# Moving the last mLSTM head ahead of the gate pairs, and keeping one output unit's partial result in SBUF, in a decoder layer's kernel

## The chip, the cores and the metric

The kernel runs on one core of a Trainium2 chip. The metric is the device time of one execution in microseconds (us). Engines are named as the profile names them: PE (TensorE, matmuls), PEld (its weight loads), DVE (VectorE), ACT (ScalarE), POOL (GpSimd), SP (SyncE, which only issues DMAs here).

## The reference, cut to what matters

One layer over 1024 positions of width 2048, all in float32: a combined projection, a sparse attention over a latent (group A), an mLSTM of four heads (group B), the output projection, and a norm.

```python
p = x @ W_in                        # 7512 columns: q, k, v, gates, indexer, ...
# group A: indexer picks the top 256 causal keys of each query,
#   h_A = softmax(q_lat . c_sel + bias) . c_sel      8 heads,  y_A = h_A * silu(z_A)
# group B, 4 heads, chunk by chunk (state C):
#   q, k = silu(conv(.)); S = (q k^T) * D
#   num = S v + inter * (q C);  C = f C + (k w)^T v
#   y_B = norm(num / den) * sigmoid(o) * silu(z)
y = concat(y_A, y_B) @ W_out        # 2048 x 2048
out = LayerNorm(alpha * x + y)
```

## The kernel before, in words

**Matmuls.** Each float32 operand is split into a high and a low part, rounded for the engine (`split`: a cast on ACT writes `..h`, a subtraction on DVE writes `..l`), and a product is three matmuls (high.high, high.low, low.high). The big projections are done as products of 2 x 2 blocks with sums of blocks, seven products for eight: `a11, a12, a22, s1..s4` are blocks and sums of the moving operand, `b11, b21, t1, t2, b22, t3, t4` those of the weights.

**Input projection.** 19 *units* (`Unit`) of two column groups each ("a pair") go through two passes over the inner dimension. A unit of either pass is 84 matmuls of 512 columns on PE. The first pass stores its part of the result in DRAM (`part_d`). The second pass loads that part into a tile `res` (L622), adds its seven products there (`add`, L676), and hands `res` on. `res` is an x_tile: one of a ring of 16 buffers (tag `xs`) that also holds the split blocks of x. A buffer is taken again when what used it last is done.

**Order of the second pass.** `sequence` lists the units head by head. For each of the four mLSTM heads there is a unit with its q and k, two *gate pairs* (output gate and SiLU gate, 256 columns) and some *other pairs*, which belong to the attention: `G_QA` pairs (queries, scaled on ACT at L893 and stored to `qa_d`) and `G_ZA` pairs (SiLU on ACT at L237, stored to `gate_a`). `shares` deals the seven other pairs out: 2, 2, 1, 2. The function `mlstm` runs the q/k unit and the convolutions, then units from its `queue` until two are left (*front* units, in which `mlstm_half` makes transposes, scores and their splits), then the two halves of the chunk recursion, each with one unit beside it. The small matmuls of a chunk (`num`, `up`) are put between the unit's 84 by `after(m)`, which holds an instruction back until the m-th of the unit's marks (a mark stands behind every sixth matmul, 14 to a unit). With heads 0 to 2 the two last units are the gate pairs, with head 3 they are two other pairs. After head 3 come `latent` (loads and splits the latent, `ch`, `cl`), `keys(0)` (`kps`: keys of attention head 0), `queries(0)` and `stores(3)` (transposes `ht` of the last head's result and its store), and then the attention, with nothing of the projection left beside them.

**Output projection.** `Product(p, c)` is one half of the inner dimension (p) for one half of the output columns (c), again seven products of 48 matmuls. There are four quarters: `unit_0` = (0,0), `unit_1` = (0,1), `unit_2` = (1,0), and a tail for the last, tile by tile of 128 rows, done in the plain way. The quarters with p = 0 store their result to DRAM (`z_d`). Those with p = 1 load x into `z` (L1375, L1490), scale it by alpha on ACT (L1376, L1491), and add `z_d` to it with an accumulating DMA of POOL (L1377, L1492). The norm works on one row tile of all four column blocks. `z`, `t_sum` (weights, also the sums `b11`, `t1` made there by accumulating DMAs) and all else named `s4(...)` share a ring of 11 buffers of 512 KB.

**Order of the instructions.** A scheduler orders each engine's instructions once, when the kernel is built, by priorities (`urgent`, `out_prio`, `high_priority`); each engine then runs its list strictly in order. SP's list is what most loads are queued in.

## Time and profile before

| | before |
|---|---|
| three runs, us | 1890.05, 1894.32, 1893.24 |
| median, us | 1893.24 |
| profiled execution: its own time, us | 1884.98 |
| profiled execution: span, us | 1882.9 |
| busy share of PE / DVE / ACT / POOL | 96% / 69% / 50% / 22% |
| mean granted clock of PE | 0.987 of full speed |

The span is the time from the first to the last instruction of the profiled execution; its own time is 2.1 us longer. It lies 8.3 us below the median of the three runs. "Granted clock" is the share of full speed that PE was given in a stretch.

### The profile page before, as it was taken

To read this page: it belongs to the slowest core of one execution; us is meant where nothing else is said; L and a number is where in the kernel's file an instruction comes from. 1 tells how busy PE (TensorE), PEld (TensorE's weight loads), DVE (VectorE), ACT (ScalarE), POOL (GpSimd) and SP (SyncE) were. 2 spreads that over 40 slices of the span, in tenths; PEclk is the share of its full clock that TensorE was granted. 3 is DMA by queue.
4 is the path that set the end of the run, shared out by engine and by line. 5 is a ranking of instruction groups with operands and counts; after the bars stand their busy time and mean duration, and the time that the engine had idled before them with its cause. 6 is when DMAs were issued, how large, how long until landed. Compare 5 with 4: busy or idle time off the path is not lost.

```text
span 1882.9 us, 25521 instructions
## 1 busy us (share of the span) xinstructions
PE 1811.0 (96%) x8740; PEld 1522.0 (81%) x8740; DVE 1295.1 (69%) x2428; ACT 949.1 (50%) x1734; POOL 411.6 (22%) x406
## 2 busy tenths in 40 slices
PE   8999999999999999999999999998799998998997
PEld 7988888888877887888888887877689987886785
DVE  6254666887788778655667676767788865555788
ACT  5334444666667633532455565546566644454421
POOL 0022121000100000011323222222344444033032
PEclk9999999999999999999999999999899999999998
DMA  7355335346545567667656755456342359699764
GB/s 269 83 167 198 118 112 154 103 117 164 149 140 144 136 174 234 211 162 220 186 161 171 208 159 165 130 166 196 109 137 93 108 124 253 194 231 259 188 185 143
DMA packets 141130, 311.74 MB, mean 166 GB/s; under 512 B 14984, under 2 KB 25992, under 8 KB 134984
## 3 DMA queue, kind: packets, MB, share of 16 engines
q1 hardware_dynamic: 114632, 259.77, 42.0%
q0 software_dynamic: 26368, 50.34, 15.7%
q8 instruction: 69, 1.13, 0.2%
q14 instruction: 61, 0.50, 0.1%
HBM read 241.77 MB, written 71.43 MB: 166 GB/s over the span
## 4 chain that ended last, share of the span: by engine, by line
PE 71%; DMA 11%; DVE 9%; issue 4%; ACT 3%; POOL 1%; SPq 1%; DVEq 0%; ACTq 0%; POOLq 0%
PE pj L667 25%; PE pj L775 5%; PE pb L667 4%; PE lps L1353 4%; PE pj L211 4%; PE pj L215 4%; PE pj L213 4%; PE pc L775 2%; DMA wraw<-wg 2%; PE pc L1353 2%; PE sc L463 2%; PE sc L464 2%; DMA z<-x 2%; DMA wraw<-wo 1%; DMA yraw<-y_d 1%
## 5 line engine op out<-in xcount | busy, mean ns | idle before, releaser
L667 PE MATMUL pj<-xh,wh 128*128 128x512 f32 x912 | 358.6, 394 | 10.0 <-DVE res L676 4.5
L667 PE MATMUL pj<-xl,wh 128*128 128x512 f32 x912 | 356.3, 391 | 0.0
L667 PE MATMUL pj<-xh,wl 128*128 128x512 f32 x912 | 352.4, 391 | 1.5 <-DVE wl L658 1.5
L654 ACT CAST wh<-wraw 128x512 fp32r<-128x512 f32 x266 | 163.3, 619 | 232.4 <-PE pj L667 111.8
L658 DVE TENSOR_TENSOR wl<-wraw,wh 128x512 fp32r<-128x512 f32 x247 | 171.8, 699 | 60.0 <-ACT wh L654 43.5
L667 PEld LDWEIGHTS pj<-xh,wh 128*128 128x128 f32 x912 | 171.7, 188 | 48.4 <-DVE res L676 6.6
L667 PEld LDWEIGHTS pj<-xh,wl 128*128 128x128 f32 x912 | 171.4, 188 | 38.8 <-DVE wl L658 4.0
L667 PEld LDWEIGHTS pj<-xl,wh 128*128 128x128 f32 x912 | 171.9, 188 | 34.2
L632 POOL DMA_DIRECT2D wraw<-wg x76 | 66.2, 872 | 487.9 <-DMA wraw<-wg 252.2
L106 DVE TENSOR_TENSOR wl<-wraw,wh 128x512 fp32r<-128x512 f32 (+4 forms) x122 | 79.2, 655 | 127.1 <-ACT wh L105 109.1
L676 DVE TENSOR_TENSOR res<-res,pj 128x512 f32<-128x512 f32 x152 | 103.1, 681 | 55.0 <-PE pj L667 43.1
L105 ACT CAST wh<-wraw 128x512 fp32r<-128x512 f32 (+4 forms) x122 | 67.7, 562 | 137.1 <-PE pj L213 57.6
L470 DVE SCALAR_TENSOR_TENSOR sc<-r,wi,sc 128x384 f32<-128x384 f32 (+2 forms) x90 | 92.0, 1045 | 45.8 <-ACT r L465 45.3
L465 ACT ACTIVATE r<-sc 128x384 f32<-128x384 f32 (+3 forms) x160 | 79.5, 523 | 79.5 <-PE sc L464 73.8
L211 PE MATMUL pj<-xh,wh 128*128 128x512 f32 x320 | 103.7, 396 | 5.7 <-ACT xh L105 5.7
L591 POOL TENSOR_TENSOR wraw<-wraw 128x512 f32<-128x512 f32 x32 | 47.6, 1487 | 258.5 <-DVE st L318 110.6
L213 PE MATMUL pj<-xl,wh 128*128 128x512 f32 x320 | 103.5, 393 | 0.0
L215 PE MATMUL pj<-xh,wl 128*128 128x512 f32 x320 | 102.8, 392 | 0.0
L501 ACT ACTIVATE junk<-sc,cand 128x512 bf16<-128x512 f32 (+2 forms) x93 | 86.5, 931 | 5.9 <-DVE cand L516 5.8
L651 POOL TENSOR_TENSOR wraw<-wraw 128x512 f32<-128x512 f32 x38 | 51.7, 1360 | 159.0 <-DVE wl L658 136.2
L1201 POOL TENSOR_TENSOR nm<-mask,tb 128x256 f32<-128x256 bf16 (+3 forms) x64 | 61.2, 974 | 108.1 <-DVE mn L1208 100.8
L504 DVE TENSOR_SCALAR_CACHE_REDUCE junk<-sc,cand 128x384 bf16<-128x384 f32 (+2 forms) x93 | 79.3, 875 | 0.7
(519 smaller groups left out, 4479.4 us busy)
## 6 DMA issues: line engine op xcount, KB each, us to landing
wraw<-wg SPq DMA_DIRECT2D x228, 256.0 KB, 4.0
wraw<-wg POOLq DMA_DIRECT2D x76, 256.0 KB, 6.0
part_d<-res SPq DMA_DIRECT2D x19, 1024.0 KB, 7.1
res<-part_d SPq DMA_DIRECT2D x19, 1024.0 KB, 7.4
wraw<-wv SPq DMA_DIRECT2D x48, 256.0 KB, 4.9
wraw<-wo SPq DMA_DIRECT2D x40, 256.0 KB, 5.0
wraw<-xT SPq DMA_DIRECT2D x32, 256.0 KB, 2.8
z_d<-z SPq DMA_DIRECT2D x16, 512.0 KB, 5.7
```

What stands on the lines that cost most here:

```text
L211: pe.matmul(ps[i], wh, xh(k, i), start=k == k_first, stop=False)
L213: pe.matmul(ps[i], wh, xl(k, i), start=False, stop=False)
L215: last_mm[0] = pe.matmul(ps[i], wl, xh(k, i), start=False, stop=k == k_last)
L465: act.activation(r[:, s], ps, AF.Relu)
L470: vec.scalar_tensor_tensor(out=sc[t], in0=r, scalar=wcol, in1=sc[t], op0=OP.mult, op1=OP.add)
L501: act.activation(junk, sc[t], AF.Sign, scale=-1.0, bias=th[:, t - 2:t - 1], accum_out=cnt[:, t - 2:t - 1])
L654: last_cast[0] = act.copy(wh, src)
L658: last_low[0] = vec.tensor_tensor(wl, src, wh.bitcast(F32), op=OP.subtract)
L667: last_mm[0] = pe.matmul(ps, w[:, k], x[:, k], start=start and k == 0 and n == 0, stop=k == 3 and n == 2, skip_group_check=True)
L676: vec.tensor_tensor(dst, dst, ps, op=OP.subtract if minus else OP.add)
L775: last_mm[0] = pe.matmul(ps[t], x[:, k, ts], y, start=start and k == 0 and n == 0, stop=k == 3 and n == 2, skip_group_check=True)
L1353: pe.matmul(ps[t], x[k][:, ts], y, start=start and k == 0 and n == 0, stop=k == 3 and n == 2, skip_group_check=True)
```

## The change

It does two things apart from each other.

In the input projection: `shares` becomes 2, 1, 1, 3. Head 3's queue ends `COVER` = 2 units early, so its chunks run beside its second gate pair and one other pair, and the last two other pairs are run after the chunks, with `latent`, `stores(3)`, `keys(0)` and `queries(0)` placed among their matmuls. The last unit's `res` is no longer an x_tile, but two buffers of the ring of 11, each loaded by a DMA of its own. `res` becomes a list of two halves throughout.

In the output projection: `unit_2` is now (1,1), on the same columns as `unit_1`, and goes on with `unit_1`'s `z` tiles in SBUF. `unit_1` loads x into them, and its first addition scales by alpha and adds in one DVE instruction. The stores to `z_d` and loads back of these columns fall away (16 transfers of 512 KB), as do the eight scalings on ACT at the start of `unit_2`. `b11` of p = 1 gets a load of its own instead of the sum left in `t_sum` (4 loads of 256 KB more), and `t_sum`'s sums are issued where the product is constructed. The tail does columns c = 0. The numbers of matmuls on PE are the same before and after; DVE has 16 instructions more, ACT 24 fewer and 2 more table loads, SP 3 DMAs fewer, POOL 8.

```diff
+COVER = 2
...
-    z_d = dp.tile([2, 8, P, 2, 512], F32, name="z_d")
+    z_d = dp.tile([8, P, 2, 512], F32, name="z_d")
...
         def __init__(self, i, g, second, X):
-            self.res = x_tile("res", (P, 2, T), F32)
+            if second and i == NU - 1:
+                self.res = [s4("res") for _ in range(2)]
+                with urgent():
+                    for n in range(2):
+                        sync.dma_start(self.res[n], part_d[i, :, n])
+                return
+            res = x_tile("res", (P, 2, T), F32)
+            self.res = [res[:, n] for n in range(2)]
             if second:
                 with urgent():
-                    sync.dma_start(self.res, part_d[i])
+                    sync.dma_start(res, part_d[i])
...
-    shares = [others[0:2], others[2:4], others[4:5], others[5:7]]
+    shares = [others[0:2], others[2:3], others[3:4], others[4:7]]
...
-        queue = [(j, sequence[j]) for j in range(first[h] + 1, (first + [NU])[h + 1])]
+        queue = [(j, sequence[j]) for j in range(first[h] + 1, (first + [NU - COVER])[h + 1])]
...
     for h in range(H_M):
         done[h] = mlstm(h)
-    ch, cl = latent()
-    k_next, q_next = keys(0), queries(0)
-    stores(H_M - 1)
+    n = len(marks)
+    for i in range(NU - COVER, NU):
+        other(sequence[i], unit(i, True, X))
+    with tc.high_priority(offset=I_PRIO):
+        ch, cl = latent()
+    with after(n + 14 * COVER - 10):
+        stores(H_M - 1)
+    with after(n + 14 * COVER - 4):
+        k_next = keys(0)
+    with tc.high_priority(offset=I_PRIO):
+        q_next = queries(0)
     ph.close()
...
-        def __init__(self, p, c):
+        def __init__(self, p, c, z=None):
             self.p, self.c = p, c
-            self.z, self.b22 = {}, {}
+            self.z, self.b22 = z or {}, {}
...
                     sync.dma_start(self.t_sum[k], a["wo"][2 * c, :, 8 * (1 - p) + k])
+                    if p:
+                        pool.dma_start(self.t_sum[k], a["wo"][2 * c + 1, :, 8 * (1 - p) + k], accum_op=OP.add)
...
+                elif name == "b11" and self.p:
+                    src = load_wo(c, k0)
...
-                if name in ("b11", "b22"):
+                if name == "b22" or name == "b11" and not self.p:
                     pool.dma_start(src, a["wo"][c + 1, :, k0], accum_op=OP.add)
...
         def block(self, i, n):
+            if self.p:
+                return
             with out_prio():
                 self.z[i, n] = [s4("z", (P, 2, 512)) for _ in range(2)]
-                if self.p:
+                if self.c:
                     for t, z in enumerate(self.z[i, n]):
...
-                        act.mul(z, z, ALPHA)
-                        pool.dma_start(z, z_d[self.c, r0:r0 + 2, :, n].rearrange("t p c -> p t c"),
-                                       accum_op=OP.add)
...
         def add(self, i, n, ps, first=False, minus=False, last=False):
+            op = OP.subtract if minus else OP.add
...
-                    if first and not self.p:
-                        if minus:
-                            act.mul(z, ps[t], -1.0)
-                        else:
-                            act.copy(z, ps[t])
+                    if not first or self.p:
+                        vec.tensor_tensor(z, z, ps[t], op=op)
+                    elif self.c:
+                        vec.scalar_tensor_tensor(out=z, in0=z, scalar=ALPHA, in1=ps[t], op0=OP.mult, op1=op)
+                    elif minus:
+                        act.mul(z, ps[t], -1.0)
                     else:
-                        vec.tensor_tensor(z, z, ps[t], op=OP.subtract if minus else OP.add)
+                        act.copy(z, ps[t])
...
-            if last and not self.p:
+            if last and not self.c:
                 for t, z in enumerate(self.z[i, n]):
...
-    unit_2 = unit_1.run(next_form(1), (1, 0))
+    unit_1.run(next_form(1))
+    unit_2 = Product(1, 1, unit_1.z)
...
-        z_1 = s4("z", (P, 2, 512))
-        sync.dma_start(z_1, a["x"][t * P:(t + 1) * P, T:].rearrange("p (n c) -> p n c", n=2))
-        act.mul(z_1, z_1, ALPHA)
-        pool.dma_start(z_1, z_d[1, t], accum_op=OP.add)
+        z = s4("z", (P, 2, 512))
+        sync.dma_start(z, a["x"][t * P:(t + 1) * P, :T].rearrange("p (n c) -> p n c", n=2))
+        act.mul(z, z, ALPHA)
+        pool.dma_start(z, z_d[t], accum_op=OP.add)
```

PE's list where the last head's chunks end, before: the head's small matmuls (`num`) follow one another, and those of the attention's first keys (`kps`) and the transposes of the head's result (`ht`) come between.

```order
L109 MATMUL num<-sh,pqh 128x258
L110 MATMUL num<-sl,pqh 128x258
L111 MATMUL num<-sh,pql 128x258
L109 MATMUL kps<-ch,wh 128x512 x2
L109 MATMUL num<-sh,pqh 128x258
L904 MATMUL ht<-ident,num 128x128
L110 MATMUL kps<-cl,wh 128x512
L111 MATMUL kps<-ch,wl 128x512
```

The same place after the change (the lines of the kernel have moved down by one here, and by ten in `Unit`): the head's last `num` matmuls stand among a unit's products `pb` and `pj`.

```order
L677 MATMUL pb<-xh,wh 128x512
L110 MATMUL num<-sh,pqh 128x258
L677 MATMUL pb<-xl,wh 128x512
L677 MATMUL pb<-xh,wl 128x512
L677 MATMUL pj<-xh,wh 128x512
L111 MATMUL num<-sl,pqh 128x258
L112 MATMUL num<-sh,pql 128x258
L677 MATMUL pj<-xl,wh 128x512
```

What moved: two units' matmuls from ahead of the chunks to beside and behind them.

SP's list in head 1, where the values of the first chunk half are loaded (`vraw`), before. `ri` are the decay rows of the front units, `wraw` weights, `qa_d<-res` stores of a queries' pair (a pair has two).

```order
L894 DMA qa_d<-res 128x1024
L629 DMA wraw<-wg 128x512 x4
L894 DMA qa_d<-res 128x1024
L913 DMA ri<-rows_d 128x2x512
L622 DMA res<-part_d 128x2048
L629 DMA wraw<-wg 128x512
L946 DMA vraw<-v_d 128x4x256
L894 DMA qa_d<-res 128x1024
```

And after, in the same head:

```order
L904 DMA qa_d<-res 128x1024
L923 DMA ri<-rows_d 128x2x512
L639 DMA wraw<-wg 128x512 x2
L904 DMA qa_d<-res 128x1024
L630 DMA res<-part_d 128x2048
L639 DMA wraw<-wg 128x512
L956 DMA vraw<-v_d 128x4x256
L639 DMA wraw<-wg 128x512 x5
```

What moved: the load of `vraw` now stands directly behind a `res` load that follows the last store of the head's one other pair; before, a second other pair's store came after it.

ACT's list where `unit_1` ends and `unit_2` begins, before: `z<-lps` is `unit_1`'s last result, `ya22h` a block of y, `wh<-wraw` the weights of `unit_2`'s products, and `z<-z` the scaling of x by alpha.

```order
L105 CAST wh<-t_sum 128x512 x4
L1386 ACTIVATE z<-lps 128x512
L105 CAST ya22h<-t 128x512 x4
L1376 ACTIVATE z<-z 128x1024 x4
L105 CAST wh<-wraw 128x512 x2
L1376 ACTIVATE z<-z 128x1024
L105 CAST wh<-wraw 128x512
L1376 ACTIVATE z<-z 128x1024
L105 CAST wh<-wraw 128x512
L1376 ACTIVATE z<-z 128x1024 x2
L105 CAST wh<-t_sum 128x512 x4
```

After (the one `z<-z` left is the tail's first):

```order
L106 CAST ys4h<-u 128x512 x4
L106 CAST wh<-t_sum 128x512 x4
L106 CAST ys3h<-t 128x512 x4
L1511 ACTIVATE z<-z 128x1024
L106 CAST wh<-wraw 128x512 x4
L106 CAST ya22h<-t 128x512 x4
L106 CAST wh<-wraw 128x512 x4
L106 CAST wh<-t_sum 128x512 x4
```

What moved: eight scalings are gone from between the weights' casts, and one of the tail's stands ahead of them.

## Rows read from the trace of the kernel before

**Rows 1.** The page: span, and busy time of each engine.

```profile
span 1882.9 us, 25521 instructions
PE 1811.0 (96%) x8740; PEld 1522.0 (81%) x8740; DVE 1295.1 (69%) x2428; ACT 949.1 (50%) x1734; POOL 411.6 (22%) x406
```

**Rows 2.** Chain that ended last: start us, length us, what.

```profile
902.34 16.32 PE pj L667 x72
...
1837.54 4.23 DMA z<-x
```

**Rows 3.** Windows: stretch and its length, busy time by engine, granted clock.

```profile
core 0: us, PE busy (x) PEld busy (x) DVE busy (x) ACT busy (x) POOL busy (x), PEclk, DMA share, GB/s
905.00:1011.49 106.49, 106.49 (x521) 89.65 (x520) 76.00 (x143) 61.98 (x100) 32.37 (x28) 1.00 0.63 177
1120.65:1226.00 105.35, 99.89 (x480) 83.35 (x479) 75.55 (x136) 58.62 (x97) 27.06 (x24) 0.98 0.55 157
1160.00:1200.00 40.00, 36.33 (x178) 30.86 (x178) 23.14 (x54) 24.22 (x41) 8.82 (x8) 0.96 0.41 110
1226.00:1304.00 78.00, 74.88 (x344) 60.41 (x343) 51.82 (x80) 44.25 (x70) 19.57 (x16) 0.98 0.57 170
1304.00:1340.00 36.00, 26.61 (x135) 21.65 (x134) 20.93 (x63) 17.65 (x33) 6.20 (x13) 0.76 0.61 203
1340.00:1360.00 20.00, 15.44 (x89) 12.99 (x88) 18.81 (x55) 14.68 (x34) 12.27 (x12) 0.91 0.17 57
1640.00:1690.00 50.00, 50.00 (x221) 41.24 (x220) 28.05 (x45) 22.57 (x41) 14.08 (x16) 1.00 0.85 216
1690.00:1730.00 40.00, 33.94 (x140) 26.58 (x139) 18.24 (x30) 18.12 (x26) 13.10 (x12) 0.96 1.07 266
```

**Rows 4.** Timeline of PE, end of head 3: start, length, instruction [idle before, releaser].

```profile
1319.72 1.22 PE L109 MATMUL kps<-ch,wh 128*128 128x512 f32 x2 [3.34 <-ACT ch L105]
...
1326.44 1.54 PE L904 MATMUL ht<-ident,num 128*128 128x128 f32 x6 [3.39 <-ACT num L1033]
```

**Rows 5.** Timeline of PE, head 2: the first chunk.

```profile
1162.42 0.58 PE L109 MATMUL num<-vh,pqh 128*128 128x258 f32 x1 [2.96 <-ACT vh L105]
```

**Rows 6.** Timeline of SP's queue, head 2, ahead of that chunk.

```profile
1147.14 0.38 SPq L238 DMA_DIRECT2D gate_a<-res  x1
...
1151.70 0.43 SPq L622 DMA_DIRECT2D res<-part_d  x1
1152.19 0.54 SPq L946 DMA_DIRECT2D vraw<-v_d  x1
```

**Rows 7.** Timeline of ACT, head 2: the cast of the values.

```profile
1161.33 1.05 ACT L105 CAST vh<-vraw 128x1024 fp32r<-128x1024 f32 x1 [6.86 <-DMA vraw<-v_d]
```

**Rows 8.** Waits of ACT at the start of unit_2: total, times, longest.

```profile
ACT z L1376 <- DMA z<-x: 16.0, 8, 2.8
```

**Rows 9.** Timeline of ACT at the start of unit_2.

```profile
1701.88 1.06 ACT L1376 ACTIVATE z<-z 128x1024 f32<-128x1024 f32 x1 [2.67 <-DMA z<-x]
...
1706.58 1.12 ACT L105 CAST wh<-wraw 128x512 fp32r<-128x512 f32 x2
```

**Rows 10.** Timeline of PE, unit_2's second product.

```profile
1707.23 0.50 PE L1353 MATMUL pb<-wh,ya12h 128*128 128x512 f32 x1 [3.16 <-ACT wh L105]
```

**Rows 11.** View of tile z: duration ns min/median/max, first and last start.

```profile
L1482 DVE SCALAR_TENSOR_TENSOR z<-z,mv_z,ln_g x24: 739/752/1793, 1798.7 to 1873.1; 128x512 f32<-128x512 f32 x24
```

**Rows 12.** Timeline of ACT at the attention's start: a table load.

```profile
1339.39 1.28 ACT L1213 ACT_TABLE_LOAD   x1
1340.69 0.51 ACT L1213 ACTIVATE lg<-lg,mn 128x256 f32<-128x256 f32 x1
```

**Rows 13.** The page, DMA issues: KB each, median us to landing.

```profile
res<-part_d SPq DMA_DIRECT2D x19, 1024.0 KB, 7.4
```

**Rows 14.** DMA issues from 1680 to 1730: KB each, median us to landing.

```profile
z<-x SPq DMA_DIRECT2D x9, 512.0 KB, 19.8
```

More of the change, by code (lines that the diff above doesn't have):

```diff
@@ L618, in __init__ @@
             self.raw = {}
-            self.res = x_tile("res", (P, 2, T), F32)
+            if second and i == NU - 1:
[6 more added lines that the diff above has]
+            self.res = [res[:, n] for n in range(2)]
             if second:
                 with urgent():
-                    sync.dma_start(self.res, part_d[i])
+                    sync.dma_start(res, part_d[i])
+            else:
+                self.kept = res
         def load(self, q, n, more=None):
@@ L684, in begin @@
             self.product(self.pa, "b11", "a11", True)
-            self.add(self.res[:, 0, 0:512], self.pa, True)
+            self.add(self.res[0][:, top], self.pa, True)
         def middle(self):
@@ L689, in middle @@
             self.product(pb, "b21", "a12", True)
-            self.add(r[:, 0, 0:512], pb)
+            self.add(r[0][:, top], pb)
             pc = pj()
             self.product(pc, "t1", "s1", True)
-            self.add(r[:, 1, 512:], pc, True)
+            self.add(r[1][:, bot], pc, True)
             self.product(pa, "t2", "s2", False)
-            self.add(r[:, 1, 0:512], pa, True, True)
+            self.add(r[1][:, top], pa, True, True)
             self.product(pc, "b22", "s4", False)
-            self.add(r[:, 1, 0:512], pc)
+            self.add(r[1][:, top], pc)
             self.product(pa, "t3", "s3", False)
-            self.add(r[:, 1, 512:], pa, minus=True)
+            self.add(r[1][:, bot], pa, minus=True)
         def end(self):
             self.product(self.pa, "t4", "a22", False)
-            self.add(self.res[:, 0, 512:], self.pa, True)
+            self.add(self.res[0][:, bot], self.pa, True)
             if not self.second:
-                sync.dma_start(part_d[self.i], self.res)
+                sync.dma_start(part_d[self.i], self.kept)
     heads = [[G_HEAD + 6 * h + 2 * j for j in range(3)] for h in range(H_M)]
     others = [G_QA + j for j in (0, 2, 4, 6)] + [G_ZA + j for j in (2, 4, 6)]
-    shares = [others[0:2], others[2:4], others[4:5], others[5:7]]
+    shares = [others[0:2], others[2:3], others[3:4], others[4:7]]
     sequence = []
@@ L879, in mlstm_gate @@
             for i, fn in enumerate((AF.Sigmoid, AF.Silu)):
-                act.activation(r[:, i], r[:, i], fn)
+                act.activation(r[i], r[i], fn)
         sg = s4("sg")
-        vec.scalar_tensor_tensor(out=sg, in0=r[:, 0], scalar=small(S_MHG + 2 * h + j), in1=r[:, 1],
+        vec.scalar_tensor_tensor(out=sg, in0=r[0], scalar=small(S_MHG + 2 * h + j), in1=r[1],
                                  op0=OP.mult, op1=OP.mult)
@@ L889, in other @@
             if g < G_QA:
-                gate_attention(g - G_ZA + i, [r[:, i, s] for s in halves], r[:, i])
+                gate_attention(g - G_ZA + i, [r[i][:, s] for s in halves], r[i])
             else:
                 with tc.high_priority(offset=I_PRIO):
-                    act.mul(r[:, i], r[:, i], -DH ** -0.5)
-                sync.dma_start(qa_d[g - G_QA + i], r[:, i])
+                    act.mul(r[i], r[i], -DH ** -0.5)
+                sync.dma_start(qa_d[g - G_QA + i], r[i])
     def y_sign(left, upper):
@@ L956, in mlstm @@
         r = unit(first[h], True, X)
-        q = conv(r[:, 0], S_CONV + 5 * h, "q")
-        k = conv(r[:, 1], S_CONV + 5 * (H_M + h), "k")
+        q = conv(r[0], S_CONV + 5 * h, "q")
+        k = conv(r[1], S_CONV + 5 * (H_M + h), "k")
         vec.tensor_scalar(k, k, DK ** -0.5, None, op0=OP.mult)
@@ L1400, in run @@
             self.block(0, 0)
-            if self.p:
-                self.block(1, 1)
             self.product(pa, "b11", "a11", True)
@@ L1409, in run @@
             then("a12")
-            if not self.p:
-                self.block(1, 1)
+            self.block(1, 1)
             pc = [bank("pc") for _ in range(4)]
@@ L1449, in last_weights @@
             return
[L1450 removed]
+        cb, k0 = {"s1": (0, 0), "s2": (1, 0), "s4": (0, 4), "s3": (1, 4)}[name]
         with out_prio():
@@ L1472, in norm @@
         refine_rsqrt(rs, mv[:, 1:2], tt)
-        for cb in (3, 0, 1, 2):
+        for cb in (3, 2, 0, 1):
             zc, g, b = z[cb], ln["ln_g", cb], ln["ln_b", cb]
@@ L1487 @@
         i, ts = t // 4, slice(t % 4 * P, (t % 4 + 1) * P)
-        z = [unit_2.z[i, n][t % 4 // 2][:, t % 2] for n in range(2)]
-        z_1 = s4("z", (P, 2, 512))
-        sync.dma_start(z_1, a["x"][t * P:(t + 1) * P, T:].rearrange("p (n c) -> p n c", n=2))
-        act.mul(z_1, z_1, ALPHA)
-        pool.dma_start(z_1, z_d[1, t], accum_op=OP.add)
+        z = s4("z", (P, 2, 512))
+        sync.dma_start(z, a["x"][t * P:(t + 1) * P, :T].rearrange("p (n c) -> p n c", n=2))
+        act.mul(z, z, ALPHA)
+        pool.dma_start(z, z_d[t], accum_op=OP.add)
         for n in range(2):
@@ L1496 @@
                 f = Y[("a11", "a12", "a21", "a22")[2 * i + kt // 4]]
-                mm3(ps, f[0][kt % 4][:, ts], f[1][kt % 4][:, ts], *W[2 + n, kt], kt == 0, kt == 7)
-            vec.tensor_tensor(z_1[:, n], z_1[:, n], ps, op=OP.add if i else OP.subtract)
-            vec.bn_stats(st[:, t, 2 + n], z_1[:, n])
-        norm(t, z + [z_1[:, 0], z_1[:, 1]])
+                mm3(ps, f[0][kt % 4][:, ts], f[1][kt % 4][:, ts], *W[n, kt], kt == 0, kt == 7)
+            vec.tensor_tensor(z[:, n], z[:, n], ps, op=OP.add if i else OP.subtract)
+            vec.bn_stats(st[:, t, n], z[:, n])
+        norm(t, [z[:, 0], z[:, 1]] + [unit_2.z[i, n][t % 4 // 2][:, t % 2] for n in range(2)])
 def layout(inputs):
```

7 lines of the change are left out of this document (3 added, 4 removed).

## Prediction

> **What bounds the kernel now.** I read the page first. PE is busy for 1811.0 of 1882.9 us [rows 1], so a change that leaves PE's work as it is can win only what PE loses. It loses in two ways: it stands idle, or it runs at a lower granted clock. The chain that ended last shows the pace at full clock: 72 matmuls of 512 columns in 16.32 us [rows 2], 0.2267 us each, so 84 x 0.2267 = 19.0 us for a unit.
>
> Then I cut the stretches that the change touches into windows [rows 3], and for each worked out *lost time* = (length - PE busy) + PE busy x (1 - clock).
>
> - 905 to 1011.49, a head with two other pairs: PE is busy throughout at clock 1.00. Lost 0.
> - 1120.65 to 1226, head 2, with one other pair: idle 5.46, clock 99.89 x 0.02 = 2.0. Lost 7.5.
> - 1226 to 1304, head 3 as far as its last unit: idle 3.12, clock 1.5. Lost 4.6.
> - 1304 to 1340, the end of head 3, where no unit is left to lie beside the chunks: idle 9.39, clock 26.61 x 0.24 = 6.39. Lost 15.8.
> - 1340 to 1360, the attention's first logits: idle 4.56, clock 1.39. Lost 5.95.
> - 1640 to 1690, inside `unit_1`: PE busy throughout at clock 1.00. Lost 0.
> - 1690 to 1730, the end of `unit_1` and the start of `unit_2`: idle 6.06, clock 1.36. Lost 7.4.
>
> The timeline says what ended the idle times. At the end of head 3 PE waits 3.34 us for a cast of the latent and 3.39 for the head's norm, each with one group of small matmuls behind it [rows 4]; the granted clock falls there, since PE has hardly worked. In head 2 it waits 2.96 for the cast of the values [rows 5], and that is a queue's doing: `res` is loaded at 1151.70 because its buffer, one of the x ring, had to be stored first (store issued at 1147.14), and `vraw` stands behind it on SP and leaves at 1152.19 [rows 6]; ACT gets it at 1161.33 after 6.86 us of waiting [rows 7]. At the start of `unit_2` ACT waits eight times, 16.0 us in all, for x [rows 8], with the casts of the weights queued behind: the cast at 1706.58 comes after such a scaling [rows 9], and PE has waited 3.16 us for it [rows 10].
>
> **The change part by part**, against the profiled execution's own time, 1884.98.
>
> *The end of head 3.* The chunks' small matmuls are moved among the second gate pair and an other pair, and two units of 19.0 us come between the chunks and the attention. PE's work is the same, but the waits of 1304 to 1340 (15.8) have matmuls beside them: each of the waits of [rows 4] is under a fifth of a unit, and the load and casts of the latent can run during 38 us of units. Bounds: 0 if the same waits only move behind the cover, 15.8 if all is covered. I take 14.3: the transposes and the first keys stand late in the cover, so I leave 1.5, about half of one wait of [rows 4]. The loss of 1340 to 1360 stays: it lies in the attention's own start.
>
> *Head 1 loses an other pair.* It gets head 2's form of before: the load of `vraw` stands behind a `res` load which waits for the only other pair's store (the second place of the order). By rows: head 2's wait of 2.96 [rows 5], and the clock that went with it, 36.33 x 0.04 = 1.45 the window 1160 to 1200 of [rows 3]. I take 4.4. Bounds: 0 (the head has room) to 7.5, all that head 2 lost.
>
> *Head 2* keeps one other pair; it shifts in the list by a unit, and its first chunk stands six matmuls earlier among the unit's. If `vraw` comes when it did, PE waits 6 x 0.2267 = 1.4 us longer. I take 1.4, between 0 and 3 (as long as its wait again).
>
> *Head 3* now also has one front unit where it had two, but that is a gate pair: its buffer is freed by a DVE product and not by a store's landing, so `res`, and `vraw` behind it, can leave earlier. Between 0 and 4.4 as in head 1; I take 1.0, near the lower end.
>
> *The start of `unit_2`.* The scalings of [rows 9] and their waits for x go, and with them what stood behind: the casts of the weights. Lost there 7.4; after it the product has its weights by loads of 256 KB with nothing ahead. I take all 7.4. What would be left: the loads of `b11`, 4 of 256 KB more on SP, but 16 transfers of 512 KB are gone, so the DMA share of 1.07 at that place [rows 3] falls. Bounds 3 to 7.4 (3 if the first cast still waits once, as in [rows 10]).
>
> *`unit_1`.* ACT loses 16 copies; DVE gets 16 instructions of the form in [rows 11], 0.752 us, 12.0 us in all. They are hidden by PE's matmuls: DVE is busy 28.05 of 50 us there with PE never waiting [rows 3], and four at a time (3.0 us) stand behind a product of 48 x 0.2267 = 10.9 us. With that cover gone they would cost up to 12.0. I take 0. x must have landed by the first addition; that is a rival, below.
>
> *Table loads.* Two more on ACT, 2 x 1.28 [rows 12], beside PE's units: 0, between 0 and 2.6.
>
> *The x ring and the tail.* The last `res` outside the ring frees one x buffer earlier for the attention; nothing in the rows waits for it, 0. The tail has the same work on other columns: 0, between -1 and 1.
>
> Sum: -14.3 + 4.4 + 1.4 + 1.0 - 7.4 = -14.9, so 1884.98 - 14.9 = 1870.1. That execution was 8.26 under the median of 1893.24 (1890.05 to 1894.32); a median of new runs should stand as far above, so **1878**.
>
> **A rule of the Trainium skill against the rows.** In the cover, SiLU (gate pairs), Sqrt (the last head's norm) and Exp alternate on ACT. A table load there took 1.28 us, and the next activation began 0.02 us after it ended (1340.69 against 1339.39 + 1.28) [rows 12]. The Trainium skill's "ScalarE: Activation LUTs", section "What ACT_TABLE_LOAD costs", gives 1283 ns for a load and about 1380 ns of drain besides, about 2.66 us for a switch. The trace agrees with the load and shows no such drain behind it. An estimate by that page: five loads in the cover would take 5 x 2.66 = 13.3 us of ACT. By the rows they take 5 x 1.28 = 6.4.
>
> **The rivals.**
>
> 1. *ACT becomes late in the cover.* Five loads, 5 x 1.28 = 6.4 us [rows 12], stand in a list that also casts weights; if PE waits for each, -14.9 + 6.4 = -8.5: 1884.7. For it: ACT's cast ends the waits at the end of head 3 [rows 4]. Against: ACT is busy 44.25 of 78 us in head 3 [rows 3], so it has slack. By the Trainium skill's figure in the section named above it would be -14.9 + 13.3, 1891.6, an estimate.
> 2. *One-pair heads cost more*: heads 1 and 3 each lose what head 2 lost in its window, 7.5, instead of 4.4 and 1.0: -14.9 + 3.1 + 6.5 = -5.3, 1887.9. Or they cost almost nothing, because the scheduler issues `vraw` in time: heads 1 to 3 at 0 gives -14.3 - 7.4 = -21.7, 1871.5, and with the attention's start also covered (-5.95) 1865.6.
> 3. *Slower: the last `res`.* Its two halves are loaded by SP into the ring of 11, whose buffers the head's chunks hold until PE has done with them. `urgent` puts DVE's first addition of that unit early in DVE's list; if the halves are late, the subtractions that make `wl` are queued behind it, ACT's next casts wait for their buffers, and PE for both. The load took 7.4 us for 1024 KB when it was free [rows 13]. PE would wait at most for the cover's unit, 19.0, and lose clock as in the window 1160 to 1200 of [rows 3] (1.7 for 19 us and some more): -14.9 + 20.7 = +5.8, 1899. It decides from a wait of 14.9 + 3.8 = 18.7 us on; below that the kernel is only less fast.
> 4. *`unit_1` waits for x.* Before, `z` was first written by ACT from PSUM; now the addition needs x. In the jam at `unit_2`'s start such a load took 19.8 us [rows 14], on a quiet path 4.2 [rows 2]. The first addition comes some 9 to 11 us after `block` (one product). At 19.8 PE would wait up to 10 us and 1.7 of clock for the first block: -3.2, 1890. Against: DMA is at share 0.85 in `unit_1` [rows 3] and PE waits for nothing there, and x can be asked for as soon as a ring buffer is free.
> 5. *One scaling is left* ahead of the casts of `unit_2`'s weights (the third place of the order). If its x lands as in [rows 14], the first product waits up to 12 us: -2.9, 1890.3. At 4.2 [rows 2] it costs nothing. Rivals 4 and 5 are one case for the chances.
> 6. *The move does nothing*: the waits of 1304 to 1340 come again behind the cover, for the attention's start needs the same keys and queries; only the output's 7.4 less heads' 6.8 is left: -0.6, 1892.6.
>
> **How the numbers follow.** What tells this kernel from no change is 0.2%, 3.8 us: faster is under 1889.5, slower over 1897.0. Chances: the forecast with its bounds 0.55 (1872 to 1885), heads that cost nothing 0.14 (1865 to 1872), rivals 1 (0.04), 2 (0.06), and 4 and 5 (0.07) where they cost 6 to 14 us 0.17 (1884 to 1892, three quarters of it under 1889.5), the move that does nothing 0.05, slower by rival 3 or by 4 and 5 together 0.09. Faster: 0.55 + 0.14 + 0.13 = 0.82; slower 0.09 and a little of rival 6, 0.10; within 0.2% the rest, 0.08. Range: 1866 to 1889, leaving out about 0.02 below and 0.18 above; the forecast's own range is 1872 to 1885.
>
> **What the profile after would show.** Right: PE busy throughout behind head 3's chunks at clock 1.00, `kps` and `ht` among a unit's matmuls, no waits above 1.5 us up to the attention; the first `num` of heads 1 and 2 waiting 3 to 4 us for `vh`; no wait for `wh` in `unit_2`; DVE's scaled additions in `unit_1` with no PE wait for `wl`. Wrong: PE idle in the cover for `wl` or `wh`, ACT waiting for `res`, DVE waiting for `z<-x` in `unit_1`, a clock under 1 in the units. The prediction would be wrong above all if the one-pair heads, whose price I have from one example, are dearer, or the last `res` comes late.

## The result, and the profile after

Four runs of the changed kernel gave a median of 1866.57 us (1861.61 to 1869.31), four of before 1891.64 (1886.01 to 1894.32): a ratio of 0.9879 with a 95% interval of 0.9858 to 0.9901. The direction was as forecast and 1866.57 is just inside the range (1866 to 1889), but 11 us under the 1878 that was predicted. The profiled execution took 1869.31, where that of before took 1884.98. So the two profiles differ by 15.7 us, and the sum of the prediction was -14.9: the sum agrees with the profiles, and the medians differ by more (25.1) than the profiles can show. The first experiment takes this up.

The page of the changed kernel, to be read against [rows 1]:

```profile
span 1867.5 us, 25484 instructions
PE 1804.2 (97%) x8740; PEld 1516.5 (81%) x8740; DVE 1314.1 (70%) x2444; ACT 934.9 (50%) x1712; POOL 402.8 (22%) x398
```

Windows of the changed kernel, cut where its own stages lie (columns as in [rows 3]): head 0, head 1, head 2, head 3 before its last chunks, the end of head 3 with the cover, the attention's first logits, then the end of `unit_1` and the start of `unit_2`:

```profile
core 0: us, PE busy (x) PEld busy (x) DVE busy (x) ACT busy (x) POOL busy (x), PEclk, DMA share, GB/s
905.00:1010.00 105.00, 104.60 (x503) 87.30 (x503) 74.14 (x140) 60.24 (x99) 31.86 (x27) 1.00 0.63 178
1010.00:1118.00 108.00, 103.67 (x504) 85.36 (x504) 81.24 (x142) 62.75 (x103) 30.48 (x26) 1.00 0.55 159
1118.00:1222.00 104.00, 96.95 (x458) 79.71 (x456) 78.41 (x136) 55.48 (x87) 24.92 (x22) 0.98 0.56 161
1222.00:1284.00 62.00, 58.70 (x285) 48.55 (x284) 45.36 (x70) 36.80 (x62) 18.89 (x16) 0.97 0.61 178
1284.00:1325.00 41.00, 41.00 (x203) 34.50 (x202) 29.69 (x73) 26.92 (x47) 6.84 (x13) 1.00 0.59 183
1325.00:1345.00 20.00, 18.73 (x120) 15.86 (x119) 18.11 (x47) 15.29 (x30) 12.08 (x13) 1.00 0.73 264
1640.00:1690.00 50.00, 44.74 (x188) 36.54 (x187) 27.12 (x44) 15.83 (x27) 17.67 (x21) 0.93 0.92 209
1690.00:1730.00 40.00, 40.00 (x178) 33.10 (x178) 27.16 (x44) 13.31 (x23) 4.35 (x5) 1.00 0.38 91
```

Lost time, worked out as in the prediction, (length - PE busy) + PE busy x (1 - clock). The clock has two digits in these rows, so the figures are rough:

| place | before, us | after, us | forecast of the difference | measured |
|---|---|---|---|---|
| head 1 | 0.7 | 4.3 | +4.4 | +3.6 |
| head 2 | 7.5 | 9.0 | +1.4 | +1.5 |
| head 3 up to its last chunks | 4.6 | 5.1 | +1.0 | +0.5 |
| end of head 3, cover | 15.8 | 0.0 | -14.3 | -15.8 |
| the attention's first logits | 5.95 | 1.3 | 0 | -4.7 |
| inside `unit_1` (1640 to 1690) | 0 | 8.4 | 0 | +8.4 |
| start of `unit_2` | 7.4 | 0 | -7.4 | -7.4 |

`unit_1` after: 50 - 44.74 + 44.74 x 0.07 = 8.4. Head 1 of before, which no row above has:

```profile
1011.00:1120.00 109.00, 108.33 (x527) 90.75 (x526) 78.26 (x145) 61.83 (x100) 30.81 (x27) 1.00 0.63 181
```

The reader should see the row 1284 to 1325: PE is busy in all 41.00 us at clock 1.00, where [rows 3] has 26.61 of 36.00 at 0.76 for the end of the same head. And the rows of 1640 and 1690: the loss at the start of `unit_2` went, and one of about the same size came some 10 us ahead of it.

The rows of 1640 and 1690 show the two places, but not all of the two units. Cut at the first matmul of each, `unit_1` and `unit_2` of before, and then of the changed kernel:

```profile
1616.60:1693.00 76.40, 76.40 (x337) 63.07 (x336) 41.00 (x65) 36.28 (x64) 17.59 (x21) 1.00 0.80 207
1693.00:1785.60 92.60, 84.37 (x350) 67.23 (x349) 58.18 (x95) 39.62 (x62) 21.48 (x23) 0.96 0.91 223
```

```profile
1607.50:1691.60 84.10, 78.84 (x337) 64.54 (x337) 49.63 (x80) 29.43 (x50) 21.57 (x25) 0.96 0.86 215
1691.60:1770.70 79.10, 79.10 (x350) 65.50 (x349) 57.93 (x95) 29.97 (x51) 7.81 (x9) 1.00 0.54 138
```

`unit_1` became 7.7 us longer and `unit_2` 13.5 shorter, that is 6 more than the 7.4 of the table. Near 4 of these 6 are one more wait of before, late in the unit, with the lower clock behind it (1.86 + 12.30 x 0.14 = 3.6); the rest the rows do not place. From the timeline of PE and the windows of before:

```profile
1773.27 0.67 PE L1353 MATMUL lps<-wh,ya22h 128*128 128x512 f32 x1 [1.86 <-DVE z L1390]
```

```profile
1773.30:1785.60 12.30, 12.30 (x47) 10.01 (x48) 12.30 (x21) 5.90 (x10) 0.93 (x2) 0.86 0.57 145
```

In the cover four table loads stand on ACT and none shows on PE. Here is one, from the timeline of ACT:

```profile
1284.78 1.28 ACT L1038 ACT_TABLE_LOAD   x1
1286.07 0.30 ACT L1038 ACTIVATE tt<-vv,eps 128x4 f32<-128x4 f32 x1
```

The activation begins 0.01 us after the load ends (1284.78 + 1.28 = 1286.06). The Trainium skill, "ScalarE: Activation LUTs", section "What ACT_TABLE_LOAD costs", puts about 1380 ns of drain beside 1283 ns of load; as in [rows 12] the trace has the load and nothing behind it that could be the drain.

The new loss begins with one wait. From the timeline of PE, and the timeline of DVE ahead of it:

```profile
1678.50 0.77 PE L1375 MATMUL lps<-wh,ya22h 128*128 128x512 f32 x1 [5.25 <-DVE z L1407]
```

```profile
1673.84 0.69 DVE L107 TENSOR_TENSOR ys4l<-u,ys4h 128x512 fp32r<-128x512 f32 x1 [1.27 <-ACT ys4h L106]
1675.26 0.69 DVE L107 TENSOR_TENSOR ys4l<-u,ys4h 128x512 fp32r<-128x512 f32 x1 [0.73 <-ACT ys4h L106]
1675.87 1.89 DVE L107 TENSOR_TENSOR wl<-t_sum,wh 128x512 fp32r<-128x512 f32 x3
1677.67 2.47 DVE L1407 TENSOR_TENSOR z<-z,lps 128x512 f32<-128x512 f32 x4
```

The last product of `unit_1` writes into the PSUM banks that DVE's addition `z<-z,lps` has yet to read. That addition stands in DVE's list behind the subtractions `ys4l`, which wait for casts of a block of y (`ys4h`), and those for its load `u<-y_d`.

### The profile page after: what moved, and what is told of

Its sections match the earlier page's. It is cut to its first block, busy times and chain, and to the rows that moved or that the text cites. A ratio compares the mean times of both kernels' runs of the same rounds, so it can differ in the third digit from the quotient of the medians.

```text
span 1867.5 us, 25484 instructions
## 1 busy us (share of the span) xinstructions
PE 1804.2 (97%) x8740; PEld 1516.5 (81%) x8740; DVE 1314.1 (70%) x2444; ACT 934.9 (50%) x1712; POOL 402.8 (22%) x398
## 3 DMA queue, kind: packets, MB, share of 16 engines
q0 software_dynamic: 24192, 46.15, 14.7%
## 5 line engine op out<-in xcount | busy, mean ns | idle before, releaser
L677 PE MATMUL pj<-xh,wh 128*128 128x512 f32 x912 | 359.1, 394 | 13.8 <-DVE res L686 6.6
```

Of the source, the lines that this page charges most:

```text
L677: last_mm[0] = pe.matmul(ps, w[:, k], x[:, k], start=start and k == 0 and n == 0, stop=k == 3 and n == 2, skip_group_check=True)
```

## The experiments

Each kernel was timed in turn with the kernel before on the same chip. For each profile two stretches are given, read from the starts of matmuls in the timeline of PE: **A** from the last matmul of the values' projection to the attention's last transpose, and **B** from the first matmul of the output projection to the kernel's last. A holds all that the input part touches, B all that the output part does. Before has A 657.5 and B 351.7; the changed kernel 645.3 and 346.1. (A ends some 19 us after B begins, so the two are not to be added.)

### The changed kernel again, and its two parts

No edit; then the diff's output part alone; then its input part alone; then the changed kernel with this edit:

```diff
-COVER = 2
+COVER = 1
-    shares = [others[0:2], others[2:3], others[3:4], others[4:7]]
+    shares = [others[0:2], others[2:4], others[4:5], others[5:7]]
```

> The changed kernel once more, against before. The profiles of before and after differ by 15.7 us (1884.98 and 1869.31), the medians by 25.1 (1891.64 and 1866.57). Theory A, the profiled pair is right about the change and the rest is spread between executions: with more rounds the difference comes near 16 to 19 us, a ratio of 0.990 to 0.992. Rival B, the profiled execution of before was an unusually good one and the gain is larger than its lost time: 22 to 27 us again, 0.986 to 0.988, and the second profile shows gains at places that the first pair does not show.

Measured: 1874.29 us against 1889.15, ratio 0.9923 (0.9906 to 0.9939), so 14.9 us; A 647.8, B 348.5. Theory A holds, even a little under its numbers. This interval and that of the first result (0.9858 to 0.9901) do not overlap, though the program is the same: before moved by 2.5 us between the two, the changed kernel by 7.7. Within either its runs lie within 8.5 us of one another. The two profiles differ in the same direction, by 2.5 us in A and 2.4 in B. What makes the difference from one such set to the next stays open (the sets of the changed kernel may have run on different chips, which was not tried); it limits what a comparison across sets says to about half a per cent.

> Only the edits of the output projection; the input projection as before. Theory A, the parts are independent and worth what the profiled pair shows from the first matmul of unit_0 on: -5.5 us (forecast -7.4), ratio 0.996 to 0.997; the wait of 3.16 us for wh in unit_2 is gone, and a wait of some 5 us for DVE at unit_1's last product stays as in the changed kernel. Rival B, the output part is worth more (-10 to -14), because the transfers that it drops also relieved other loads. Rival C, the output part alone is worth nothing, and gains only when PE gets there earlier.

Measured: 0.9971 (0.9958 to 0.9984), 5.5 us; A 657.5 as before, B 346.1. Theory A holds, rival B falls by the size, and rival C falls: PE gets to `unit_1` no earlier than in before, and the wait at its end is there all the same. From the view of waits of PE, 1640 to 1740:

```profile
PE lps L1357 <- DVE z L1389: 4.4, 1, 4.4
```

> Only the edits of the input projection; the output as before. Theory A: -10 us, ratio 0.994 to 0.995 (forecast -7.5): the end of head 3 has no waits, one-pair heads lose some 3 us each to DVE's wl behind the wait for ri. Rival B: -15 to -20, 0.990 to 0.992, with the output worth only the rest. Rival C: the last res or the cover costs and it is worth under 5 us.

Measured: 0.9949 (0.9935 to 0.9963), 9.6 us, and 0.9927 (0.9908 to 0.9946) when it was repeated as a pair with a later run. A 645.8 and 647.4, B 353.4 and 349.4. Theory A holds; the parts add: 5.5 + 9.6 = 15.1 against 14.9 together, all on one chip.

> The changed kernel with the old shares 2, 2, 1, 2 and one unit of cover instead of two: head 1 keeps two front pairs, head 3 has one front gate pair as in the changed kernel. Theory A, a one-pair head costs 2 to 4 us: head 1's waits for vh (1.98, 0.56, 0.40) and for wl go, but one unit (19 us) does not cover the latent, the keys and the transposes, some 5 to 8 us of waits and half clock come back at the attention's start; 2 to 5 us slower than the changed kernel. Rival B, one unit is cover enough: 2 to 4 us faster than the changed kernel, no wait above 1.5 us at the transition. Rival C: the same as the changed kernel within 2 us, both prices small.

Measured: 0.9952 (0.9937 to 0.9967), 5.5 us slower than the changed kernel's second ratio; A 654.9, so 7 to 10 us of the input part's gain is gone. Theory A, at the upper end of its 2 to 5 us or just over it. Rivals B and C fall. Head 1 waits for `vh` no more, but one unit does not cover the end. From the timeline of PE and the windows:

```profile
1325.90 1.33 PE L914 MATMUL ht<-ident,num 128*128 128x128 f32 x5 [7.24 <-ACT num L1043]
```

```profile
1290.00:1330.00 40.00, 30.07 (x145) 25.13 (x144) 26.02 (x65) 22.34 (x40) 8.05 (x14) 0.89 0.64 206
```

9.93 + 30.07 x 0.11 = 13.2 us are lost there, nearly the 15.8 of [rows 3], and over half of it is one wait. The second unit of cover is what pays, more than it costs that head 1 gives up a pair.

### What was left: two late loads

In the changed kernel two things in the profile looked alike: a load that leaves late, and behind it an in-order list of DVE in which PE's next operand is queued. One is the wait above. The other is in the heads. What PE waited for in heads 1 to 3, 1010 to 1284, in the changed kernel (the four largest):

```profile
PE pj L677 <- DVE res L686: 5.7, 6, 2.0
PE pj L677 <- DVE wl L668: 5.2, 2, 2.8
PE num L110 <- ACT vh L106: 2.0, 1, 2.0
PE pj L677 <- ACT wh L664: 0.8, 2, 0.6
```

The wait for `vh` is in head 1, those for `wl` are in heads 2 and 3, and 4.3 of the 5.7 us for `res` are in head 2. From the timelines of DVE and PE in head 2:

```profile
1144.70 0.69 DVE L947 TENSOR_TENSOR pq<-q,ri 128x512 f32<-128x512 f32 x1 [3.83 <-DMA ri<-rows_d]
...
1146.51 0.68 DVE L668 TENSOR_TENSOR wl<-wraw,wh 128x512 fp32r<-128x512 f32 x1
```

```profile
1147.24 0.80 PE L677 MATMUL pj<-xh,wl 128*128 128x512 f32 x1 [2.76 <-DVE wl L668]
```

In head 3 DVE waits for `ri` too (5.14 us, up to 1241.67), but PE's wait for `wl` (2.48, up to 1253.30) comes 11 us later, so the link is less direct there.

The edit for the first, on top of the changed kernel (`last_y` is the last `u<-y_d` of the form s4):

```diff
             with urgent():
                 for k in range(4):
                     sync.dma_start(self.t_sum[k], a["wo"][2 * c, :, 8 * (1 - p) + k])
-                    if p:
-                        pool.dma_start(self.t_sum[k], a["wo"][2 * c + 1, :, 8 * (1 - p) + k], accum_op=OP.add)
+            if p:
+                with out_prio(), tc.issue_after(last_y[0].ins):
+                    for k in range(4):
+                        pool.dma_start(self.t_sum[k], a["wo"][2 * c + 1, :, 8 * (1 - p) + k], accum_op=OP.add)
```

> The changed kernel, but the accumulating DMAs that make t_sum's sums for unit_2 are issued behind the last accumulating load of y (u<-y_d) instead of where the product is constructed. In the runs with the output edits PE waits 4.4 to 5.3 us for DVE at unit_1's last product; in those without it does not. Theory: two of these DMAs stand in POOL's list ahead of u<-y_d, which leaves 7 us later, the casts ys4h and the subtractions ys4l behind it come 9 us later, and DVE's additions to z are queued behind them. Then the wait falls under 1.5 us and the kernel is 3 to 6 us faster than the changed kernel, ratio to before near 0.990. Rival: the loads of x in unit_1 delay u<-y_d (the DMA engines are full there); then the wait stays at 3 to 5 us and the time is the same. Rival 2: the wait only moves to unit_2's t1, which needs t_sum: no gain, and a wait of 3 us for wh there.

Measured: 0.9873 (0.9852 to 0.9893), 9.4 us under the changed kernel's 0.9923; B 341.5, 4.6 to 7 us less than with the sums early. The 0.9923 is from another chip, and against the first result's 0.9879 little would be left, so the run to compare with is `res_in_x` below: the changed kernel but for one place in memory, on the same chip with the same runs of before, 0.9910. Against it the edit is worth 7.3 us (1870.43 to 1863.10), more than the theory's 3 to 6. The timeline of POOL in before, in the changed kernel, and then with the edit:

```profile
1663.04 3.54 POOL L1140 DMA_DIRECT2D u<-y_d  x4
```

```profile
1653.09 0.86 POOL L1343 DMA_DIRECT2D t_sum<-wo  x1 [1.39 <-DMA t_sum<-wo]
1655.06 0.86 POOL L1343 DMA_DIRECT2D t_sum<-wo  x1 [1.11 <-DMA t_sum<-wo]
1656.42 1.87 POOL L1364 DMA_DIRECT2D wraw<-wo  x2 [0.49 <-issue]
1658.69 0.86 POOL L1158 DMA_DIRECT2D u<-y_d  x1 [0.40 <-issue]
...
1662.58 0.86 POOL L1158 DMA_DIRECT2D u<-y_d  x1 [0.41 <-DVE wl L107]
```

```profile
1651.83 0.86 POOL L1158 DMA_DIRECT2D u<-y_d  x1 [0.76 <-DVE ys2l L107]
...
1655.41 0.86 POOL L1158 DMA_DIRECT2D u<-y_d  x1 [0.41 <-DMA wraw<-wo]
1656.74 0.86 POOL L1347 DMA_DIRECT2D t_sum<-wo  x1 [0.47 <-PE pc L1379]
```

From the second of these to the third the four loads of y leave 7 us earlier, but `unit_1` begins 4 us earlier in this execution, at 1603.6 and not 1607.5. Counted from its first matmul they leave at 48.3 to 51.8 us with the edit, at 51.2 to 55.0 in the changed kernel, and at 46.4 to 48.5 in before, whose `unit_1` begins at 1616.6: the edit wins 3 us of the 5 to 6.5 that the change had cost them (the 7 and 9 us that were expected are too much). The wait falls by 3.3 us to 1.9, a little more than the 1.5 that the theory allowed, and `unit_1` takes 80.3 us: half of what it had lost. So the sums' place is shown to make about half of the loss. Of that half x's loads are not the cause, since x is loaded as before; whether they, or something else that the change put into `unit_1`, make the other half was not tried. The second rival falls: the view of waits of PE, 1640 to 1740, has no other line than this, with the edit:

```profile
PE lps L1379 <- DVE z L1411: 1.9, 1, 1.9
```

The edit for the second, on top of the changed kernel:

```diff
     def mlstm_half(...):
-        ri = s4("ri", (P, 2, 512))
-        sync.dma_start(ri, bcast_rows(rows_d[h, :, s]))
+        ri = ris[half]
...
     def mlstm(h):
         if h:
             stores(h - 1)
+        ris = []
+        with urgent():
+            for s in halves:
+                ris.append(s4("ri", (P, 2, 512)))
+                sync.dma_start(ris[-1], bcast_rows(rows_d[h, :, s]))
```

> The changed kernel, but both halves' decay rows ri are loaded ahead of a head's front units. In the changed kernel the one-pair heads 2 and 3 wait 2.5 to 2.9 us each for wl, which stands on DVE behind an instruction that waits 3.8 us for ri; head 1 waits for vh. Theory: these two waits fall under 0.7 us, with half clock that follows them some 5 to 8 us less in all, ratio to before 0.988 to 0.990. Rival: DVE and ACT are just full in a single front unit that has both halves' work (table loads among it); the waits stay at 1.5 us or more each, and the time within 2 us. Rival 2: the two buffers of the ring held longer delay vraw and the waits for vh grow: slower by 2 to 5 us.

Measured: 0.9845 (0.9828 to 0.9863), 14.7 us under the changed kernel's 0.9923 and 12.5 under `res_in_x`; A 633.4, 12 to 14 less. The theory's direction holds and its size was low by about half: not only the two waits for `wl` are gone, but those for `vh` and most of those for `res`; some for `wh` came instead. Both rivals fall. The same view of waits as above has, with the edit, only:

```profile
PE pj L677 <- ACT wh L664: 2.8, 3, 1.5
PE pj L677 <- DVE res L686: 0.8, 2, 0.6
```

Both edits together:

> Both edits of the two runs before this one. If they are independent, their gains add: 8 to 13 us under the changed kernel, ratio to before 0.985 to 0.988. If each was a rival's case, the same as the changed kernel.

Measured: 1850.62 us, 0.9808 (0.9788 to 0.9829); A 633.4, B 341.0. The gains add: against 0.9923 it is 9.4 + 14.7 = 24.1 by the ratios and 21.7 measured, against `res_in_x` 7.3 + 12.5 = 19.8 and 19.8 measured. That is more than the 8 to 13 expected, as each gain was. This is the fastest version of the study, 37.7 us under before.

The changed kernel with the last unit's `res` as all others':

```diff
-            if second and i == NU - 1:
-                self.res = [s4("res") for _ in range(2)]
-                with urgent():
-                    for n in range(2):
-                        sync.dma_start(self.res[n], part_d[i, :, n])
-                return
             res = x_tile("res", (P, 2, T), F32)
```

> The changed kernel with the last unit's res in x's memory again, as for all other units. Forecast: nothing hangs on it, within 2 us of the changed kernel (a ratio to before near 0.992). Rival: the attention's first tiles, which take x's memory, wait for the last unit's result and its SiLU and store; then the first logits come 5 to 8 us later, and PE waits there at half clock: 0.996.

Measured: 0.9910 (0.9890 to 0.9931); A 647.2, B 346.9. Its ratio is 0.0013 under the second of the changed kernel and its profile agrees, so the forecast holds, as far as two sets can be compared: where the last `res` lies is worth nothing that can be measured.

### Whether the change made the heads' price

The theory behind the next three was that the change, with one front unit in three heads, had made most of what the early `ri` gave back.

First the edit on `ri` in the kernel before, by itself:

> The kernel before, with one edit alone: both halves' decay rows ri are loaded ahead of a head's front units. With the edit, the changed kernel became some 15 us faster (0.9845 against 0.9923 of before). Theory: the change made that price, with one front unit in three heads instead of one; before has one such head, and its waits there (2.96 and 1.25 in head 2, 1.98 in head 3) are not all for ri, so the edit brings before 2 to 6 us, ratio 0.997 to 0.999. Rival: ri was late in every head and the price was there already; then before gains 10 us or more, 0.995 or less, and the forecast's price of the one-pair heads (6.8 us in all) was not the step that was off. Rival 2: nothing, 1.000, since the wait for vh in head 2 is SP's queue.

Measured: 1877.21 us against 1888.67, 0.9927 (0.9904 to 0.9950); A 645.5, 12 less than before. The rival holds and the theory falls: before paid nearly as much for the late `ri` (11.5 us by the medians, 13.8 by the ratio). Windows of before with this edit, for head 2 and head 3 (they answer to the rows of 1120.65 and 1226 in [rows 3]):

```profile
1120.00:1226.00 106.00, 104.49 (x514) 87.03 (x512) 82.64 (x147) 62.28 (x100) 31.46 (x27) 1.00 0.61 177
1226.00:1296.00 70.00, 70.00 (x335) 58.16 (x334) 46.70 (x74) 39.78 (x67) 16.06 (x14) 1.00 0.54 162
```

Head 2 loses 1.5 instead of 7.5, head 3 up to the end of its last unit (at 1295 in this run) nothing instead of 4.6, and no matmul waits for `vh`. So rival 2 of this expectation falls with the theory. The wait of [rows 5] was laid to SP's queue, and that was right; but the order in that queue can be changed. From the timeline of SP with the edit, in head 2:

```profile
1148.63 0.54 SPq L945 DMA_DIRECT2D vraw<-v_d  x1
...
1156.88 0.37 SPq L622 DMA_DIRECT2D res<-part_d  x1
```

The load of `vraw` now stands ahead of the `res` load that waits for the store, where in [rows 6] it stands behind it. So the edit does two things, an earlier `ri` for DVE and another order on SP; what each is worth was not separated.

Then the input part alone as a pair, without the edit on `ri` and with it:

> Only the edits of the input projection, once more as it is (0.9949 the first time), for a pair on one chip with the run that has the edit on ri: 0.994 to 0.996.

Measured: 0.9927 (0.9908 to 0.9946), as told above.

> Only the edits of the input projection, with ri loaded early as above. Theory: the move is worth, without the price of the heads with one front unit, what the end of head 3 lost (15.8) and more of the attention's start: with the edit's own gain on before, 0.986 to 0.989 against before, 11 to 17 us under the run with the input edits alone. Rival: the gain on the changed kernel came from the output part being reached earlier; then 0.992 to 0.995 here.

Measured: 0.9875 (0.9852 to 0.9898); A 629.6, B 352.1. In the band of the theory against before, but 10 us under its pair, just short of the 11 to 17 expected. So the move of the head is worth 10 to 14 us without the early `ri` (0.9949 and 0.9927) and, against before with the same edit, 0.9927 - 0.9875 = 0.0052, 10 us, with it: the two edits add, nearly or in full, and the early `ri` does not make the move worth more.

Last the output part alone, with the sums of `t_sum` issued late as above:

> Only the edits of the output projection, with t_sum's sums issued behind the last u<-y_d. From the first matmul of unit_0 to the last of the kernel PE takes 349 to 354 us in the profiles without the output edits, 345 to 349 with them, and 341 in the two with the sums issued late. Theory: the output part alone is worth 5 us as it is (0.9971 measured) and 10 to 12 us with the sums late: 0.994 to 0.995, the stretch 341 us, the wait at unit_1's last product under 2 us. Rival: the gain of the late sums needs PE to get there earlier; then 0.996 to 0.998 and the wait of over 4 us stays.

Measured: 0.9935 (0.9921 to 0.9950), 12.3 us; B 341.5; the wait at `unit_1`'s end 2.2 us:

```profile
PE lps L1361 <- DVE z L1393: 2.2, 1, 2.2
```

The theory holds but for the wait, which it put under 2 us. The output part with the sums late is worth 12 us (10.2 by B), and as the change has it 5.5. `unit_1` is 3.8 us shorter here than in the output part with the sums early, as it is in the changed kernel; the edit's gain in the medians (6.8 and 7.3 us) is larger than that, and the rest is not located.

## Why the prediction was right, and where its terms were off

**The end of head 3: right.** Forecast -14.3 of 15.8; all 15.8 went. `kps` and `ht` stand among a unit's matmuls as the order showed, and with one unit of cover instead of two most of the loss came back (13.2 us).

**The attention's start: mis-sized.** Forecast 0, since the wait was taken to lie in the attention itself; 4.7 of 5.95 us went in the first profile and nearly as much in the second (1.1 left). The prediction had this only as a part of rival 2. That the attention's first keys and casts are ready before PE gets there, since they run beside units, fits this but was not tried by itself. One part of it was clock (1.39 of the 5.95): in the row 1325 to 1345 it is 1.00.

**The one-pair heads: right in size to within 4 us, in part in the mechanism.** Heads 1, 2 and 3 were forecast at +4.4, +1.4 and +1.0, 6.8 in all; the first profile gives +3.6, +1.5 and +0.5, the second +5.2, +2.7 and +2.4, so 5.6 and 10.3. Head 1 does wait for `vh`, 1.98 us where 3 to 4 were forecast; head 2, forecast to wait for it longer than before, does not wait for it at all, but for `res` and `wl`, and head 3 for `wl`. The load of `ri` behind these waits, which the prediction did not name, was late in before too: with `ri` early head 2 of before loses 1.5 us, so the one example of the price was mostly a price of this load and of SP's order, not of a head with one other pair.

**The start of `unit_2`: right at its place, but one edit beside it was not priced.** All of the 7.4 went there, and some 6 us more in the rest of `unit_2`, so the unit's gain of 13.5 lies beyond the term's upper bound. Against that `unit_1` became 7.7 us longer. The prediction told of the loads of `b11` and let the sums of `t_sum`, which the change issues where the product is constructed, pass without a price. Two of them stand in POOL's list ahead of the loads of y, and putting them behind gives 3.8 of the 7.7 back; the other half stays open. That the output part's -5.5 lies inside the bounds of the term (-3 to -7.4) is luck: a gain of 6 and a loss of 7.7, both unforeseen, nearly cancel. With the sums late, the same edits are worth -12.3.

**`unit_1`'s DVE work, the table loads, x's loads, the last `res`: nothing was forecast, and nothing is shown to be theirs.** From 1600 us to the end PE waits once, at the end of `unit_1`, and the timeline lays that to `ys4l`, not to the scaled additions nor to x; for the half of the loss that stays with the sums late this was not tried. Rival 1 (ACT late in the cover) falls by the row 1284 to 1325, rival 3 by the same row and by the run with `res` in x's memory, rival 4 since no wait of PE stands in `unit_1` before 1678, rival 5 by the row of 1690, rival 6 by the cover. Of rival 2, heads that cost all that head 2 lost, the second profile comes nearest (10.3 of the 16.4 that its numbers add to). Its other half, heads that cost nothing and a covered start of the attention, gives 1865.6, close to the median; but the heads did cost, so the number is near by accident.

**The sum and the medians.** By the terms: forecast -14.9, by the profiled executions -15.7, by the parts timed alone -15.1, by the repeat of the whole -14.9. That it comes out so closely is luck in part: the attention's start (-4.7), the rest of `unit_2` (-6) and the loss in `unit_1` (+7.7) were all put at nothing and offset each other, and the two profiles of the changed kernel differ by 4.7 us themselves. The step that failed is the last one, "a median of new runs should stand as far above": the profiled execution of before was faster than each of the four runs timed with it, and that of after the slowest of its four, and the first set of after lay 7.7 us below the second. Part of this lies ahead of the stretches that the change touches: stretch A begins at 880.2 us in the profile of before and at 880.6 to 884.5 in the thirteen others. One profiled execution's distance to a median is not a property of the kernel to be carried over.

## What to carry to other kernels

Work that is moved to give a stage something to hide behind is worth what that stage lost, clock included, less what the place that it was taken from now loses; the loss can be read off as idle time plus what busy time at a lower clock costs. Count the stage after it too: here 4.7 us went there. Every DMA that an edit issues earlier on an in-order queue is an edit of its own: ask which load it passes, which casts wait for that load, and what is queued behind those on the next engine. And when a wait seems to be a queue's doing, see whether a small load that could have left long ago is what holds the queue's order: here it was worth nearly as much as the whole change.

## What was not expected of the hardware

The same program gave medians of 1866.57 and 1874.29 us in two sets of runs, with intervals against before that do not overlap, while each set lay within 8.5 us; no run shows why.

A short wait can cost more than its own length, and does not always. In the changed kernel one wait of 5.25 us made `unit_1` 7.7 us longer: PE had been busy at full clock up to it, and the row 1640 to 1690 has a mean clock of 0.93. With the sums late a wait of 1.9 us made it 3.9 us longer than in before; with the output part alone and the sums late a wait of 2.2 us made it only 2.5 longer, and the clock stayed up. The windows around the wait in these two runs:

```profile
1669.00:1690.00 21.00, 19.05 (x78) 15.36 (x77) 14.50 (x24) 8.74 (x15) 2.62 (x3) 0.92 0.76 205
1680.00:1702.00 22.00, 19.82 (x88) 16.10 (x87) 16.31 (x27) 10.74 (x19) 2.62 (x3) 1.00 0.87 217
```
